# A decoder trunk's block attention: the causal mask added by VectorE, and two query blocks' scores in one stretch

## The chip, the cores and the metric

The kernel runs on one core of a Trainium2 chip. The metric is the device time of one execution in microseconds (us); the median of several executions is compared, and less is better. The core's engines work side by side: TensorE (PE in the profile, its weight loads PEld) multiplies matrices into PSUM; VectorE (DVE) and ScalarE (ACT) do elementwise work and reductions; GpSimd (POOL) and SyncE (SP) mostly issue transfers. Each engine takes its instructions in the order in which the program gives them.

## What is computed

Two layers of a decoder trunk on 512 positions of width 1024. In each, a normalised and modulated input goes through one combined projection; three token mixers follow (pooling, a short convolution, block attention), gated and merged; then an output projection, a second normalisation and a gated feed-forward part. The change is in the block attention: 8 heads of 64, blocks of 256 positions, so a query sees its own block causally, and, if it lies in the second block, the first ("past") block when the routing test admits it:

```python
gate = jnp.einsum('bhqd,bhnd->bhqn', q_i.astype(jnp.float32), kmean)
past = jnp.arange(nb) < blk
gate = jnp.where(past, gate, NEG)
...
s_sel = jnp.where(valid[..., None], s_sel, NEG)
s_own = jnp.where(kpos[None, :] <= qpos[:, None], s_own, NEG)
p = jax.nn.softmax(jnp.concatenate([s_sel, s_own], axis=-1), axis=-1)
```

## The kernel before

TensorE works in a split form: each operand is held as a rounded high part and a low remainder, and `mm3` (L159) issues three matmuls per product. Weights come by DMA as raw tiles (three buffers); ScalarE rounds them to `whi` (L327), VectorE subtracts to get `wlo` (L330), and `next_w` (L351) keeps three or four such pieces ahead of TensorE.

The order of TensorE's work is written out by hand: `matmul` and `transpose` (L150 to L157) keep the program's order. The other engines' instructions are ordered when the program is built, by when their inputs are expected. Side work is woven into the main matmuls by a clock: every 2048 columns of `mm3` are a `tick` (L135), that is four products of 512 columns, twelve main matmuls. At a tick, generators in `fibers` count down and go on, and a queue `bulk` of side tasks gets `bulk_rate` of credit (L906 sets 0.35 for the attention). The tasks there are mostly dots for the modulation (`ada_dot`, L376: a weight row block of 128x1024 times a vector, on VectorE, with one load of 512 KB each).

Attention (`attention`, L661) runs as such a generator beside the gate projections. For each of 4 head pairs it transposes queries and keys (L573) and starts four units, one per 128 queries (`unit`, L580; i is 0 to 3). A unit has three stages:

1. Scores (L584 to L592): a PSUM tile of two banks, one per head (`ps_pair`, two buffers). Two bf16 matmuls of an identity with a mask tile write the mask into the diagonal 128 columns; six matmuls (three split terms, two heads on 64 rows each) add the scores, over 256 columns for units 0 and 1, 384 for unit 2 and 512 for unit 3. Then the softmax on VectorE and ScalarE. For units 0 and 1: maximum (L598), times the scale (L599), two exponentials with sums (L601), reciprocal (L621), scaling of the weights (L623). For units 2 and 3 also the sum over the past block for the routing test (L606 to L608), a maximum over the past (L609) and over the own block (L611), and four exponentials (L616, L618).
2. After `WAIT` ticks (2 for unit 0, else 3): the weights are transposed by TensorE (L632), rounded and split (L634, L635).
3. Two ticks later: the product with the values (L644) and its evacuation (L649 to L654).

The next unit starts `GAP` ticks (2 or 3) after the one before, so two units overlap. With more than 256 keys the third stage's result goes into the unit's own score tile (L641), which is then held until stage 3 has been read.

Of the kernel before, what the change touches and what calls it, by code (L numbers as in the profile page):

```python
# [27 lines left out]
HD = 64  # L28
PAIRS = HEADS // 2
TT = S // P  # L30
# [5 lines left out]
BLOCK = 256  # L36
# [3 lines left out]
NEG = -1e30  # L40
SCALE = 1.0 / math.sqrt(HD)
# [38 lines left out]
def hybrid_trunk(ctx, tc, xT, ws, ada, cols, pool_w, qk_w, crow, pos, con, out):  # L80
    nc = tc.nc
    V, A, T = nc.vector, nc.scalar, nc.tensor

    const = ctx.enter_context(tc.tile_pool(name="const", bufs=1))
# [20 lines left out]

    def ps_pair():
        return psum.tile([P, 2, S], F32, tag="pair", name=nm("pair"), bufs=2)
# [4 lines left out]
    def sm(shape, dt=F32, tag="sm", bufs=8):  # L112
        return small.tile(shape, dt, tag=tag, name=nm(tag), bufs=bufs)
# [8 lines left out]
    bulk_rate, credit = [0.0], [0.0]  # L122
# [27 lines left out]
    def matmul(*a, **k):  # L150
        tc.keep_in_program_order(T.matmul(*a, **k))  # L151
# [44 lines left out]
    ident = const.tile([P, P], F32, name="ident")  # L196
    make_identity(nc, ident)
    ones = const.tile([P, P], F32, name="ones")
    nc.gpsimd.memset(ones, 1.0)
    ident16 = const.tile([P, P], BF16, name="ident16")  # L200
    nc.gpsimd.tensor_copy(ident16, ident)
    mask = const.tile([P, P], BF16, name="mask")
    nc.gpsimd.memset(mask, 0.0)
    nc.gpsimd.affine_select(out=mask, in_=mask, compare_op=ALU.is_ge, fill=NEG,
                            base=0, pattern=[[-1, P]], channel_multiplier=1)
    epst = const.tile([P, 1], F32, name="epst")
    nc.gpsimd.memset(epst, EPS)

    A.activation(csil, csil, AF.Silu)

# [366 lines left out]
    GAP = (2, 3, 3, 3)  # L577
    WAIT = (2, 3, 3, 3)

    def unit(hp, i, q, k, v, y, nrq, prq):  # L580

        w = P * (i + 1)
        wm = max(w, BLOCK)
        s = ps_pair()  # L584

        for a in range(2):
            matmul(s[:, a, i * P:w], ident16, mask, start=True, stop=True)
        for z, (qa, ka) in enumerate(((0, 0), (0, 1), (1, 0))):
            for a in range(2):
                r = slice(a * HD, (a + 1) * HD)  # L590
                matmul(s[:, a, :wm], q[qa][r, i * P:(i + 1) * P], k[ka][r, :wm],
                       start=False, stop=(z == 2), skip_group_check=True)  # L592
        cell = lambda: sm([P, 2], tag="asm", bufs=16)
        nsc, sc = nrq[:, i, 2 * hp:2 * hp + 2], prq[:, i, 2 * hp:2 * hp + 2]
        m, nb, den = cell(), cell(), cell()
        pr = [tmp() for _ in range(2)]
        if w <= BLOCK:
            V.tensor_reduce(m, s[:, :, :w], axis=AX.X, op=ALU.max)  # L598
            V.tensor_mul(nb, m, nsc)  # L599
            for a in range(2):  # L600
                A.activation(pr[a][:, :w], s[:, a, :w], AF.Exp, bias=nb[:, a:a + 1],  # L601
                             scale=sc[:, a:a + 1], accum_out=den[:, a:a + 1])
        else:

            gs, pen, mp, nbp, d2 = cell(), cell(), cell(), cell(), cell()
            V.tensor_reduce(gs, s[:, :, :BLOCK], axis=AX.X, op=ALU.add)  # L606
            V.tensor_mul(gs, gs, sc)
            V.tensor_scalar(pen, gs, NEG * BLOCK * SCALE, NEG, op0=ALU.is_lt, op1=ALU.mult)  # L608
            V.tensor_reduce(mp, s[:, :, :BLOCK], axis=AX.X, op=ALU.max)  # L609
            V.tensor_add(mp, mp, pen)  # L610
            V.tensor_reduce(m, s[:, :, BLOCK:w], axis=AX.X, op=ALU.max)  # L611
            V.tensor_max(m, m, mp)
            V.tensor_mul(nb, m, nsc)
            V.tensor_add(nbp, nb, pen)
            for a in range(2):
                A.activation(pr[a][:, :BLOCK], s[:, a, :BLOCK], AF.Exp, bias=nbp[:, a:a + 1],  # L616
                             scale=sc[:, a:a + 1], accum_out=den[:, a:a + 1])
                A.activation(pr[a][:, BLOCK:w], s[:, a, BLOCK:w], AF.Exp, bias=nb[:, a:a + 1],  # L618
                             scale=sc[:, a:a + 1], accum_out=d2[:, a:a + 1])
            V.tensor_add(den, den, d2)  # L620
        V.reciprocal(den, den)  # L621
# [5 lines left out]
        for aa in ([0, 1],) if i < 2 else ([0], [1]):  # L627
            n = len(aa)
# [17 lines left out]
        c = slice(i * P, (i + 1) * P)  # L646
# [73 lines left out]
    for l in range(L):  # L720
# [7 lines left out]
        for n, (k, lo, hi) in enumerate([(k, 0, S) for k in range(KT)] if l == 0 else HALVES + REST):  # L728
# [17 lines left out]
            w = held[k]  # L746
# [94 lines left out]
        for j in range(2):  # L841
# [8 lines left out]
            z = bigt(F32)  # L850
# [33 lines left out]
        for t in range(TT):  # L884
            for half in range(2):
                src = v_ps[t][:, half * BLOCK:(half + 1) * BLOCK].rearrange("p (n d) -> p n d", d=HD)
                o = v[half][t]
# [15 lines left out]

        if l == 0:
            bulk.extend(ada_tasks(l, (SC2, SH2), True))
        bulk_rate[0] = 0.35  # L906
        ahead_now[0] = 3

        def gate():
# [197 lines left out]
        for part, (along, single, pairs) in enumerate(PARTS):  # L1107
# [18 lines left out]
            for _ in range(single):  # L1126
                wg = next_w()
                g = ps_mm()
                feature_tile(g, wg)
                u = ps_mm()  # L1130
# [135 lines left out]
```

## Time and profile before

| | before |
|---|---|
| median of 3 runs | 1458.94 us (1458.75 to 1459.29) |
| the profiled execution | 1458.56 us, span of its trace 1456.8 us |
| mask matmuls | 64, some 224 ns each from start to end |
| attention stage of layer 0, of layer 1 | from about 134.6 us, from about 851 us |

The profile is one execution. Its span runs from the first to the last instruction of the program; the execution's own time is a little longer. A row of the timeline gives the start in us from the span's start, the length in us, the engine, the source line, the operation, what is written from what, the shape and the number of like instructions that follow each other. TensorE's matmuls are pipelined: a matmul's length is longer than its distance to the next one's start, so costs are read from the distance between starts. All matmuls have one of two lines, L151 (`matmul`) and L157 (`transpose`), so they are told apart by their tiles: `pair<-mask,ident` the mask, `pair<-big,big` on 64 rows the scores, `mm<-ident,tmp` the transposes of weights, `mm<-ident,w` those of queries and keys, `mm<-big,whi` and `mm<-big,wlo` the main matmuls.

### The profile page before, as it was taken

Reading aid. Unit: us, or ns where it says so; the run is one execution under the profiler, and the core shown is the slowest. Engines: PE = TensorE matmul, PEld = TensorE weight load, DVE = VectorE, ACT = ScalarE, POOL = GpSimd, SP = SyncE. Lnnn points to the kernel's source line nnn. Section 1 sums busy time; section 2 is a strip of 40 time slices with the busy share of each in tenths; the row PEclk is TensorE's granted clock in tenths of the full one; section 3 lists DMA queues with packets and bytes.
Section 4 is the critical chain, followed back from the end, with each engine's and each line's share of the span. In section 5 each row is a group of like instructions: output and inputs, shape, how many; then the busy total and the mean of one; then the engine's idle time right before and its main releaser. Section 6 shows DMA issues by size and latency. Waiting matters only on the chain.

```text
span 1456.8 us, 21945 instructions
## 1 busy us (share of the span) xinstructions
PE 1449.7 (100%) x8443; PEld 1267.1 (87%) x8443; DVE 1053.3 (72%) x1855; ACT 665.5 (46%) x1138; POOL 105.9 (7%) x157
## 2 busy tenths in 40 slices
PE   9999999999999999999999999999999999999998
PEld 7888888788989998989988888888889889989997
DVE  7988888748686767677797866776587757657663
ACT  4634555443554452535444355555335525434450
POOL 0000000001100311210000000000010102111200
PEclk9999999999999999999999999999999999999999
DMA  9645334445436666756545422222463436636522
GB/s 352 225 137 173 123 109 137 138 159 142 109 127 211 194 174 203 187 151 199 191 148 177 157 79 73 73 74 101 154 194 88 135 124 164 183 100 190 136 87 84
DMA packets 84409, 217.19 MB, mean 149 GB/s; under 512 B 10832, under 2 KB 23760, under 8 KB 84304
## 3 DMA queue, kind: packets, MB, share of 16 engines
q1 hardware_dynamic: 67456, 177.37, 35.7%
q0 software_dynamic: 16128, 37.76, 11.9%
q8 instruction: 66, 1.08, 0.3%
q10 hardware_dynamic: 720, 0.66, 0.1%
q14 instruction: 39, 0.32, 0.1%
HBM read 213.65 MB, written 2.10 MB: 148 GB/s over the span
## 4 chain that ended last, share of the span: by engine, by line
PE 96%; DMA 2%; DVE 1%; ACT 0%; issue 0%; SPq 0%; POOL 0%
PE mm L151 82%; PE pair L151 13%; PE mm L157 2%; DMA w<-in_ws 1%; DMA w<-in_ada 0%; DMA x<-in_xT 0%; DVE w L376 0%; DVE wlo L330 0%; ACT whi L327 0%; DVE big L504 0%; SPq L190 0%; DVE tmp L497 0%; ACT big L501 0%; DVE w L635 0%; DVE big L702 0%
## 5 line engine op out<-in xcount | busy, mean ns | idle before, releaser
L151 PE MATMUL mm<-big,whi 128*128 128x512 f32 (+1 forms) x4362 | 1079.9, 339 | 0.3 <-DVE w L635 0.2
L151 PEld LDWEIGHTS mm<-big,whi 128*128 128x128 f32 x4362 | 745.3, 190 | 84.8 <-DVE w L635 0.6
L151 PE MATMUL mm<-big,wlo 128*128 128x512 f32 (+1 forms) x2181 | 735.9, 337 | 0.0
L151 PEld LDWEIGHTS mm<-big,wlo 128*128 128x128 f32 x2181 | 413.8, 190 | 44.5
L327 ACT ACTIVATE whi<-raw 128x1024 fp32r<-128x1024 f32 (+2 forms) x240 | 248.8, 1039 | 277.8 <-PE mm L151 193.7
L330 DVE TENSOR_TENSOR wlo<-raw,whi 128x1024 fp32r<-128x1024 f32 (+2 forms) x240 | 283.8, 1192 | 53.7 <-ACT whi L327 53.4
L327 ACT ACTIVATE whi<-w 128x1024 fp32r<-128x1024 f32 x72 | 76.2, 1058 | 149.1 <-PE mm L151 88.7
L958 DVE SCALAR_TENSOR_TENSOR x<-mm,mod,x 128x512 f32<-128x512 f32 (+1 forms) x90 | 61.8, 688 | 79.6 <-PE mm L151 79.5
L256 POOL DMA_DIRECT2D w<-in_ws x72 | 48.2, 678 | 961.7 <-DVE w L376 390.3
L330 DVE TENSOR_TENSOR wlo<-w,whi 128x1024 fp32r<-128x1024 f32 x72 | 86.7, 1220 | 32.0 <-ACT whi L327 31.4
L376 DVE SCALAR_TENSOR_TENSOR w<-w,csil 128x1024 f32<-128x1024 f32 x80 | 95.8, 1219 | 14.0 <-DMA w<-in_ada 13.8
L151 PE MATMUL pair<-whi,big 128*128 128x512 f32 x224 | 76.7, 390 | 0.0
L258 POOL DMA_DIRECT2D w<-in_ws x72 | 64.6, 937 | 152.1 <-DMA w<-in_ws 137.4
L151 PE MATMUL pair<-big,whi 128*128 128x256 f32 (+1 forms) x376 | 74.0, 294 | 0.0
L151 PEld LDWEIGHTS pair<-big,whi 128*128 128x128 f32 x376 | 60.4, 191 | 2.2
L151 PE MATMUL mm<-whi,big 128*128 128x512 f32 x160 | 57.2, 394 | 1.4 <-ACT big L501 1.1
L151 PE MATMUL pair<-big,wlo 128*128 128x256 f32 (+1 forms) x188 | 55.3, 294 | 0.0
L918 DVE SCALAR_TENSOR_TENSOR big<-big,mm 128x512 f32<-128x512 f32 x48 | 32.6, 683 | 26.5 <-PE mm L151 26.1
L151 PEld LDWEIGHTS pair<-whi,big 128*128 128x128 f32 x224 | 42.1, 188 | 8.6
L515 DVE TENSOR_TENSOR big<-tmp,big 128x512 fp32r<-128x512 f32 x48 | 33.1, 691 | 21.7 <-ACT big L514 20.7
L514 ACT ACTIVATE big<-tmp 128x512 fp32r<-128x512 f32 x48 | 29.8, 622 | 35.2 <-DVE tmp L1100 12.8
L151 PE MATMUL pair<-wlo,big 128*128 128x512 f32 x112 | 43.7, 390 | 0.0
(192 smaller groups left out, 1241.1 us busy)
## 6 DMA issues: line engine op xcount, KB each, us to landing
raw<-in_ws SPq DMA_DIRECT2D x146, 512.0 KB, 3.4
w<-in_ada SPq DMA_DIRECT2D x80, 512.0 KB, 4.9
w<-in_ws POOLq DMA_DIRECT2D x144, 256.0 KB, 4.6
raw<-in_ws SPq DMA_DIRECT2D x64, 256.0 KB, 3.9
raw<-in_ws SPq DMA_DIRECT2D x24, 384.0 KB, 3.4
raw<-in_ada SPq DMA_DIRECT2D x16, 512.0 KB, 3.3
raw<-in_ws SPq DMA_DIRECT2D x16, 448.0 KB, 5.5
raw<-in_ws SPq DMA_DIRECT2D x36, 128.0 KB, 2.8
```

The lines of the kernel that those rows point to most:

```text
L151: tc.keep_in_program_order(T.matmul(*a, **k))
L157: tc.keep_in_program_order(T.transpose(*a))
L256: nc.gpsimd.dma_start(dst, self.source(0, 1))
L258: nc.gpsimd.dma_start(dst, self.source(*other), accum_op=ALU.add)
L327: A.activation(hi[:, :n], raw[:, :n], AF.Copy)
L330: ins = V.tensor_sub(lo[:, :n], raw[:, :n], f32(hi)[:, :n])
L376: return V.scalar_tensor_tensor(aw, aw, 1.0, csil, op0=ALU.mult, op1=ALU.mult, accum_out=mod[l][:, part, j:j + 1])
L514: A.activation(hi, src, AF.Copy)
L515: last_split[0] = V.tensor_sub(lo, src, f32(hi))
L918: V.scalar_tensor_tensor(sg, sg, 1.0, branch, op0=ALU.add, op1=ALU.mult)
L958: V.scalar_tensor_tensor(x[k][:, lo:hi], src, mod[l][:, part, k:k + 1], x[k][:, lo:hi], op0=ALU.mult, op1=ALU.add)
```

## The change

The bf16 identity and mask become one f32 mask in SBUF, and a column `fill` with the routing threshold is added. Unit 0 issues the scores of units 0 and 1 in one stretch of twelve matmuls into one pair tile (columns 0 to 255 of each bank for unit 0, 256 to 511 for unit 1), and one VectorE addition puts the mask onto both diagonal blocks. Unit 1 then takes its half of that tile. Units 2 and 3 issue their six score matmuls without the mask; their softmax does the past block's sum, maximum and test first, then adds the mask to the diagonal block, and the own block's exponentials stand ahead of the past's. The bulk rate in the attention goes from 0.35 to 0.27.

```diff
-    ident16 = const.tile([P, P], BF16, name="ident16")
-    nc.gpsimd.tensor_copy(ident16, ident)
-    mask = const.tile([P, P], BF16, name="mask")
+    mask = const.tile([P, P], F32, name="mask")
...
+    fill = const.tile([P, 1], F32, name="fill")
+    nc.gpsimd.memset(fill, NEG * BLOCK * SCALE)
...
-        wm = max(w, BLOCK)
-        s = ps_pair()
-
-        for a in range(2):
-            matmul(s[:, a, i * P:w], ident16, mask, start=True, stop=True)
-        for z, (qa, ka) in enumerate(((0, 0), (0, 1), (1, 0))):
-            for a in range(2):
-                r = slice(a * HD, (a + 1) * HD)
-                matmul(s[:, a, :wm], q[qa][r, i * P:(i + 1) * P], k[ka][r, :wm],
-                       start=False, stop=(z == 2), skip_group_check=True)
+
+        def scores(o, i, n):
+            for z, (qa, ka) in enumerate(((0, 0), (0, 1), (1, 0))):
+                for a in range(2):
+                    r = slice(a * HD, (a + 1) * HD)
+                    matmul(o[:, a], q[qa][r, i * P:(i + 1) * P], k[ka][r, :n], start=(z == 0), stop=(z == 2))
+
+
+        if i == 0:
+            s = first_two[hp] = ps_pair()
+            for u in range(2):
+                scores(s[:, :, u * BLOCK:(u + 1) * BLOCK], u, BLOCK)
+            diag = s.rearrange("p a (g c) -> p a g c", c=P)[:, :, 0:TT:TT - 1]
+            V.tensor_add(diag, diag, mask.unsqueeze(1).unsqueeze(1).to_broadcast([P, 2, 2, P]))
+        elif i == 1:
+            s = first_two.pop(hp)[:, :, BLOCK:]
+        else:
+            s = ps_pair()
+            scores(s[:, :, :w], i, w)
...
-            gs, pen, mp, nbp, d2 = cell(), cell(), cell(), cell(), cell()
-            V.tensor_reduce(gs, s[:, :, :BLOCK], axis=AX.X, op=ALU.add)
-            V.tensor_mul(gs, gs, sc)
-            V.tensor_scalar(pen, gs, NEG * BLOCK * SCALE, NEG, op0=ALU.is_lt, op1=ALU.mult)
-            V.tensor_reduce(mp, s[:, :, :BLOCK], axis=AX.X, op=ALU.max)
-            V.tensor_add(mp, mp, pen)
-            V.tensor_reduce(m, s[:, :, BLOCK:w], axis=AX.X, op=ALU.max)
-            V.tensor_max(m, m, mp)
-            V.tensor_mul(nb, m, nsc)
-            V.tensor_add(nbp, nb, pen)
+            past, own, diag = s[:, :, :BLOCK], s[:, :, BLOCK:w], s[:, :, i * P:w]
+            gs, under, mp, nbp, d2 = cell(), cell(), cell(), cell(), cell()
+            V.tensor_reduce(gs, past, axis=AX.X, op=ALU.add)
+            V.tensor_reduce(mp, past, axis=AX.X, op=ALU.max)
             for a in range(2):
-                A.activation(pr[a][:, :BLOCK], s[:, a, :BLOCK], AF.Exp, bias=nbp[:, a:a + 1],
+                V.scalar_tensor_tensor(under[:, a:a + 1], gs[:, a:a + 1], sc[:, a:a + 1], fill,
+                                       op0=ALU.mult, op1=ALU.is_lt)
+            V.tensor_add(diag, diag, mask.unsqueeze(1).to_broadcast([P, 2, P]))
+            V.scalar_tensor_tensor(mp, under, NEG, mp, op0=ALU.mult, op1=ALU.add)
+            V.tensor_reduce(m, own, axis=AX.X, op=ALU.max)
+            for a in range(2):
+                V.scalar_tensor_tensor(nb[:, a:a + 1], m[:, a:a + 1], mp[:, a:a + 1], nsc[:, a:a + 1],
+                                       op0=ALU.max, op1=ALU.mult)
+            V.scalar_tensor_tensor(nbp, under, NEG, nb, op0=ALU.mult, op1=ALU.add)
+            for a in range(2):
+                A.activation(pr[a][:, BLOCK:w], own[:, a], AF.Exp, bias=nb[:, a:a + 1],
                              scale=sc[:, a:a + 1], accum_out=den[:, a:a + 1])
-                A.activation(pr[a][:, BLOCK:w], s[:, a, BLOCK:w], AF.Exp, bias=nb[:, a:a + 1],
+            for a in range(2):
+                A.activation(pr[a][:, :BLOCK], past[:, a], AF.Exp, bias=nbp[:, a:a + 1],
                              scale=sc[:, a:a + 1], accum_out=d2[:, a:a + 1])
...
-        bulk_rate[0] = 0.35
+        bulk_rate[0] = 0.27
```

More of the change, by code (lines that the diff above doesn't have):

```diff
@@ L578, in hybrid_trunk @@
     WAIT = (2, 3, 3, 3)
+    first_two = {}
     def unit(hp, i, q, k, v, y, nrq, prq):
         w = P * (i + 1)
-        wm = max(w, BLOCK)
-        s = ps_pair()
-        for a in range(2):
-            matmul(s[:, a, i * P:w], ident16, mask, start=True, stop=True)
-        for z, (qa, ka) in enumerate(((0, 0), (0, 1), (1, 0))):
-            for a in range(2):
-                r = slice(a * HD, (a + 1) * HD)
-                matmul(s[:, a, :wm], q[qa][r, i * P:(i + 1) * P], k[ka][r, :wm],
-                       start=False, stop=(z == 2), skip_group_check=True)
+        def scores(o, i, n):
[14 more added lines that the diff above has]
+            scores(s[:, :, :w], i, w)
         cell = lambda: sm([P, 2], tag="asm", bufs=16)
```

## The prediction

> **What bounds the kernel now.** First the profile's page: its span, its busy shares and the chain that ended last; then who TensorE waited for, and the two stretches that hold the attention of the two layers.
>
> ```profile
> span 1456.8 us, 21945 instructions
> PE 1449.7 (100%) x8443; PEld 1267.1 (87%) x8443; DVE 1053.3 (72%) x1855; ACT 665.5 (46%) x1138; POOL 105.9 (7%) x157
> ...
> PE 96%; DMA 2%; DVE 1%; ACT 0%; issue 0%; SPq 0%; POOL 0%
> ...
> PE pair L151 <- POOL ones L199: 1.1, 1, 1.1
> ...
> PE mm L151 <- DVE big L504: 0.2, 1, 0.2
> ...
> 125.00:300.00 175.00, 175.00 (x921) 141.18 (x920) 138.51 (x326) 92.69 (x208) 0.00 (x0) 1.00 0.37 127
> 835.00:1010.00 175.00, 174.80 (x911) 140.62 (x910) 123.31 (x292) 90.51 (x202) 0.00 (x0) 1.00 0.22 78
> ```
>
> The last two rows give, after the stretch and its length, the busy time of PE, PEld, DVE, ACT and POOL, and then the granted clock. TensorE has work in 1449.7 of 1456.8 us, 96% of the chain is TensorE, and the rows of its waits, of which the first and the last of five stand here, run from 1.1 us down to 0.2. In both attentions it never rests. So what leaves TensorE's own sequence leaves the span, as long as nothing that it needs comes late; VectorE has 138.5 of 175 us taken in layer 0 and 123.3 in layer 1, and can take more if it is not in a hurry.
>
> "Busy" is modelled, so I take TensorE's costs from the starts of consecutive matmuls. The rows are start, length, operation, count. One normal step first, then the first head pair's unit 0, unit 1 with unit 0's transposes, and two blocks of transposes that stand alone.
>
> ```profile
> 31.76 2.72 PE mm L151 x12
> ...
> 134.41 0.39 PE L151 MATMUL mm<-big,wlo 128*128 128x512 f32 x1
> 134.64 0.28 PE L151 MATMUL pair<-mask,ident 128*128 128x128 bf16 x2
> 134.85 0.62 PE L151 MATMUL pair<-big,big 64*128 64x256 f32 x6
> 135.40 0.74 PE L151 MATMUL mm<-big,whi 128*128 128x512 f32 x2
> 135.98 0.40 PE L151 MATMUL mm<-big,wlo 128*128 128x512 f32 x1
> ...
> 140.79 0.39 PE L151 MATMUL mm<-big,wlo 128*128 128x512 f32 x1
> ...
> 141.78 0.44 PE L157 MATMUL mm<-ident,tmp 128*128 128x128 f32 x2
> 141.98 0.71 PE L151 MATMUL mm<-big,whi 128*128 128x512 f32 x2
> 142.52 0.39 PE L151 MATMUL mm<-big,wlo 128*128 128x512 f32 x1
> ...
> 160.87 0.96 PE L151 MATMUL pair<-big,big 64*128 64x512 f32 x6
> 161.76 0.87 PE L157 MATMUL mm<-ident,tmp 128*128 128x128 f32 x6
> ...
> 164.98 0.39 PE L151 MATMUL mm<-big,wlo 128*128 128x512 f32 x1
> 165.21 0.60 PE L157 MATMUL mm<-ident,w 128*128 128x128 f32 x4
> 165.57 0.70 PE L151 MATMUL mm<-big,whi 128*128 128x512 f32 x2
> 166.10 0.39 PE L151 MATMUL mm<-big,wlo 128*128 128x512 f32 x1
> ...
> 172.29 1.03 PE L157 MATMUL mm<-ident,tmp 128*128 128x128 f32 x8
> 173.08 0.71 PE L151 MATMUL mm<-big,whi 128*128 128x512 f32 x2
> ```
>
> A main matmul takes 2.72/12 = 0.227 us. An interruption costs what lies between its neighbours beyond one step, and what the next two main matmuls take beyond 0.45:
> - unit 0 (mask and 6 score matmuls): 135.40-134.41-0.23 = 0.76, and 0.58-0.45 = 0.13; together 0.89.
> - unit 1 with unit 0's 2 transposes: 141.98-140.79-0.23 = 0.96, and 0.09; 1.05.
> - the two mask matmuls: 134.85-134.64 = 0.21.
> - six more score matmuls of 256 columns: the six at 512 take 161.76-160.87 = 0.89, those at 256 take 0.55; 256 more columns in each cost 0.34 (the two heads' row halves run side by side, so this is three streams, 0.113 each).
> - transposes alone: four cost 165.57-164.98-0.23 = 0.36 and 0.08 after them, 0.44; eight take 173.08-172.29 = 0.79 ahead of that tail (from a main matmul to the first transpose is a normal step, 164.98 to 165.21). So 0.11 each, and two cost 0.44-0.22 = 0.22.
>
> **The change, part by part.**
>
> (1) The mask leaves TensorE: 32 units lose two matmuls, 0.21 us each. Not all of it need be gained, as three rows of the timeline show, in which single matmuls are cut out of the groups above:
>
> ```profile
> 134.71 0.22 PE L151 MATMUL pair<-mask,ident 128*128 128x128 bf16 x1
> 134.85 0.38 PE L151 MATMUL pair<-big,big 64*128 64x256 f32 x2
> ...
> 135.19 0.28 PE L151 MATMUL pair<-big,big 64*128 64x256 f32 x2
> ```
>
> From the second mask matmul to the first scores are 0.14 to 0.15 us, where one mask matmul follows the other after 0.07: some 0.09 passes with nothing streaming. From the last scores to the next main matmul (135.40) are 0.21, against a stream of 0.11: again 0.09 to 0.10. From a main matmul to the mask are 0.23, a normal step: nothing is lost. The lost 0.09 comes where the array goes from 128 rows to 64 or back, not where the type changes. After the change a main matmul (128 rows) is followed by scores (64 rows), a pairing that the trace doesn't have. Its cost beyond a normal step lies between 0 (a stream of 0.227 us cannot be cut short) and, if the scores need all that the mask now takes, 0.21; I take the 0.09 of the two nearest rows. The gain is then 0.21-0.09 = 0.12 per unit, 0.21 at one end and 0 at the other. The Trainium skill, TensorEngine Tiling (Array Packing), section Tiling Modes, says that changing the tiling mode drains TensorE; by that rule the mask bears a cost now that the scores will bear afterwards, the trace agrees with its 0.09 us at both changes of rows, and the sum below would be 6.8 us; without the rule, 9.0.
>
> (2) Unit 1's scores move into unit 0's stretch. Before, units 0 and 1 with unit 0's transposes cost 0.89+1.05 = 1.94 us per head pair. After: one stretch of 0.89-0.21+0.09+0.34 = 1.11 and two transposes alone, 0.22: 1.33. That is 0.61 less (0.70 without the 0.09), masks included, for 8 head pairs: 4.9 us (5.6). Units 2 and 3 gain by (1) alone: 16 times 0.12 = 1.9 us (16 times 0.21 = 3.4). TensorE's sequence is **6.8 us** shorter (9.0; and if the scores took all 0.21, 8 times 1.94-(0.89+0.34+0.22) = 3.9).
>
> (3) VectorE takes the mask, and here a wait can arise: the transposes of a unit's weights wait for L623, and TensorE runs in order, so whatever stands behind them waits too. The nearest rows for the new additions are VectorE's additions out of PSUM; below them, unit 0's chain with its exponentials on ScalarE, and the tightest chain, of a unit 3.
>
> ```profile
> 143.08 0.41 DVE L635 TENSOR_TENSOR w<-mm,w 128x256 fp32r<-128x256 f32 x1
> 153.56 0.68 DVE L635 TENSOR_TENSOR w<-mm,w 128x512 fp32r<-128x512 f32 x1
> ...
> 135.71 1.22 DVE L376 SCALAR_TENSOR_TENSOR raw<-raw,csil 128x1024 f32<-128x1024 f32 x1
> 136.86 0.42 DVE L598 TENSOR_REDUCE asm<-pair 128x2 f32<-128x256 f32 x1
> 137.31 0.16 DVE L599 TENSOR_TENSOR asm<-asm,nrq 128x2 f32<-128x2 f32 x1
> ...
> 137.60 0.45 ACT L601 ACTIVATE tmp<-pair,asm,nrq 128x128 f32<-128x128 f32 x1
> 138.38 0.21 ACT L601 ACTIVATION_READ_ACCUMULATOR tmp<-pair,asm,nrq 128x1 f32 x1
> ...
> 139.22 0.48 DVE L623 TENSOR_SCALAR tmp<-tmp,asm 128x128 f32<-128x128 f32 x2
> ...
> 256.14 0.88 DVE L623 TENSOR_SCALAR tmp<-tmp,asm 128x512 f32<-128x512 f32 x2
> 256.79 1.04 PE L157 MATMUL mm<-ident,tmp 128*128 128x128 f32 x8
> ```
>
> Units 0 and 1: one addition over 512 elements, 0.68 us. Units 2 and 3: one over 256, 0.41 us. The rest of the softmax keeps its two or three reductions; small operations of 0.15 to 0.17 are exchanged for about as many (multiply, test, add, maximum, multiply, add: 6; now 2 tests, 2 combined updates, 2 combined maxima: 6). VectorE gains 4(0.68+2 times 0.41) = 6 us per layer, 138.5 to some 145 of 170. That hides as long as each chain meets its deadline.
>
> Unit 0's deadline comes closer from two sides. Its chain grows by 0.68, and, in the order in which the changed program's instructions stand on VectorE, unit 1's maximum (512 elements, as many as the addition, so 0.6 to 0.7) comes ahead of unit 0's L623; and unit 1's scores no longer stand ahead of unit 0's transposes on TensorE (0.76, as 134.64 to 135.40 for unit 0's; 0.34 of it is now spent in the stretch before). For the first head pair, whose L623 ends at 139.70 against transposes at 141.78, a margin of 2.1 us: in the new order a dot (L376, 135.71 to 136.86, 1.15) also stands between its maximum and L599. Addition 136.86 to 137.56, maximum to 138.0, dot to 139.2, L599 to 139.4, the exponentials, as now about 1.0 from the first's start to the second's sum (137.60 to 138.59), to 140.45, reciprocal 140.6, unit 1's maximum 141.2, L623's first half 141.5. TensorE arrives at about 141.78-0.61 = 141.2. That is a stall of 0.3 to 0.5 us. The three other pairs of layer 0 have no such dot at that place, and I expect none there.
>
> Units 2 and 3 have three ticks of main matmuls (3 times 2.72 us) for their chain. The tightest of the 32 blocks of transposes is in the third pair: the first half of L623 ends at about 256.14+0.44 = 256.6, the transposes start at 256.79: 0.2 us to spare. Their chain grows by 0.41, but the lower rate (part 5) takes one dot of 1.15 out of just this stretch in the new order. For it and the next tightest I allow 0.2 us in all. Stalls: **0.6 us**. The bounds: 0, as now; and 3.8, if all eight units 2 and 3 of layer 0 paid their whole growth (3.3) on top of unit 0's 0.5.
>
> (4) The own block's exponentials ahead of the past's: the same four instructions, ScalarE (92.7 of 175 us) has room; the first starts when nb is there, one operation of 0.16 earlier. Costed at nothing; without that room it is 0.16 in 16 units, 2.6 us, and only where a unit has no margin.
>
> (5) The bulk rate: 16 dots stand in layer 0's attention now. At 0.27 for 0.35 all 16 still come before the flush behind the gates in the new order, the last three some 25 to 30 us later than now, in stretches with no unit. They and their loads are the same in number, and no transfer is added; SyncE's queue is only passed in another order. Nothing.
>
> ```profile
> L376 DVE SCALAR_TENSOR_TENSOR raw<-raw,csil x16: 1211/1216/1226, 133.4 to 276.8; 128x1024 f32<-128x1024 f32 x16
> ```
>
> (6) Pair tiles: three instead of four are taken per head pair from two buffers. The next pair's first scores need unit 2's tile, as they do now, and unit 3's the one of units 0 and 1, read long before. Nothing. POOL builds one constant less a copy, at the start: nothing.
>
> Sum: -6.8+0.6 = -6.2 us on the profiled execution's 1458.56 (its span 1456.8 and 1.8 around it): 1452.4. The median, 1458.94, lies 0.4 above that execution, so I put the median at **1452.6**. About 0.2% (2.9 us) is what a measurement of this kernel can tell from no change.
>
> **Rivals.**
> - *No drain without the mask* (chance 0.22): a main matmul passes into scores as it now passes into the mask, in one step. For it: 134.41 to 134.64 is a normal step. Against it: both changes of rows in the trace lose 0.09. Then -9.0+0.6: 1450.5 (1449.9 without stalls).
> - *The chain eats a part* (0.17): VectorE's order puts a weight split or a dot of 1.2 us into one chain after the other, in layer 0 above all. For it: the margin of 0.2 us and unit 0 above. Against it: layer 1 has no dots there. With 2 to 4 us of stalls 1454.1 to 1456.1.
> - *Slower* (0.06): TensorE waits at the transposes of almost every unit of layer 0, as every wait of VectorE for an exponential also holds up the weight splits queued behind it, and these the next unit. For it: VectorE's queue is in order. To lose 6.8 and 2.9 more, growth has to exceed the margin by 9.7/16 = 0.6 us in each of the 16 units; the first pair's unit 0, with its 2.1, would have to grow by 2.7, against 1.3 and a dot worked out. It decides where VectorE's queue is full (layer 0); then 1462 or more.
> - *The mask's time gives nothing* (0.05): the scores' weights are loaded in the 0.21 us that the mask takes and would need them anyway. For it: the load of a score's weights begins only there. Only the joined stretches are gained, 3.9-0.6: 1455.6; and with the chain eating as above 1457 to 1459.
>
> **How the numbers follow.** Forecast 0.50 (1451.5 to 1453.5), no drain 0.22, partly eaten 0.17, mask's time not gained 0.05, slower 0.06. The range goes from the gain without drain and stalls (1458.9-9.0 = 1449.9, and 0.4 for the spread of the runs, 1449.5) to the bound of 3.8 us of stalls, 1455.9; no more than the last two cases and a little lies outside. Faster by over 0.2% (under 1456.0): 0.50+0.22 and 0.15 of the third, 0.87; within 0.2% 0.07; slower by over 0.2% 0.06.
>
> **What would show it.** No row of mask and ident on TensorE; from a main matmul to the first scores 0.32 us between starts (forecast) or 0.23 (no drain); the stretch of 12 scores costing 1.1 us and two transposes alone 0.22; TensorE's waits with a row for VectorE's L623 of about 0.6 us in layer 0. A sum of those waits of 3 us and more, or idle TensorE in layer 1's attention, would make it wrong.

## The result, and the profile after

The changed kernel takes **1453.05 us** (median of 6 runs, 1452.58 to 1454.23), the kernel before 1458.74 us (6 runs, 1458.61 to 1459.29): a ratio of 0.9961, 95% interval 0.9948 to 0.9974. The forecast was 1452.6, the range 1449.5 to 1455.9. The profiled execution took 1453.40 us.

The profile's page of the changed kernel: span, busy shares, and the chain that ended last by engine.

```profile
span 1451.6 us, 21853 instructions
...
PE 1443.5 (99%) x8379; PEld 1263.2 (87%) x8379; DVE 1062.9 (73%) x1879; ACT 664.0 (46%) x1138; POOL 105.5 (7%) x157
...
PE 95%; DVE 2%; DMA 1%; ACT 1%; issue 0%; SPq 0%; ACTq 0%
```

PE has 8379 matmuls where it had 8443, the 64 of the mask less, and is still the bound. VectorE's part of the chain went from 1% to 2%. Whom TensorE waited for (us in all, times, longest):

```profile
...
PE mm L157 <- DVE w L651: 0.8, 1, 0.8
...
```

This row is new: a transpose (L157) waited 0.8 us for L651, which is the split of transposed weights (L635 before). There is none for L639, the scaling of the weights (L623 before), the place where I had looked for the stalls. The same two stretches as before, busy time of PE, PEld, DVE, ACT, POOL:

```profile
125.00:300.00 175.00, 174.20 (x898) 141.07 (x897) 142.21 (x333) 92.04 (x209) 0.00 (x0) 1.00 0.36 121
835.00:1010.00 175.00, 174.91 (x896) 141.53 (x895) 128.72 (x310) 91.81 (x211) 0.00 (x0) 1.00 0.24 82
```

In layer 0 TensorE now rests for 0.8 of 175 us. VectorE took up 5.4 us in layer 1 (123.3 to 128.7) and 3.7 in layer 0; 6 were forecast. In layer 0 the lower rate moved two dots, 2.5 us, to behind the end of this stretch (the last dot starts at 313.4 for 276.8), so 6.2 came there too. Now the timeline of TensorE and VectorE: the joined stretch, the addition of the mask, the first pair's unit 0, and the place of the new wait.

```profile
134.79 0.39 PE L151 MATMUL mm<-big,wlo 128*128 128x512 f32 x1
135.11 0.97 PE L151 MATMUL pair<-big,big 64*128 64x256 f32 x12
136.01 0.74 PE L151 MATMUL mm<-big,whi 128*128 128x512 f32 x2
136.59 0.40 PE L151 MATMUL mm<-big,wlo 128*128 128x512 f32 x1
137.20 0.70 DVE L598 TENSOR_TENSOR pair<-pair,mask 128x512 f32<-128x512 f32 x1
...
141.29 0.47 DVE L639 TENSOR_SCALAR tmp<-tmp,asm 128x128 f32<-128x128 f32 x2
141.40 0.39 PE L151 MATMUL mm<-big,wlo 128*128 128x512 f32 x1
141.62 0.52 PE L157 MATMUL mm<-ident,tmp 128*128 128x128 f32 x2
141.91 0.71 PE L151 MATMUL mm<-big,whi 128*128 128x512 f32 x2
...
162.24 1.22 DVE L376 SCALAR_TENSOR_TENSOR raw<-raw,csil 128x1024 f32<-128x1024 f32 x1
163.38 0.69 DVE L618 TENSOR_REDUCE asm<-pair 128x2 f32<-128x512 f32 x1
163.99 0.68 DVE L619 TENSOR_REDUCE asm<-pair 128x2 f32<-128x512 f32 x1
164.58 0.34 DVE L621 SCALAR_TENSOR_TENSOR asm<-asm,nrq,fill 128x1 f32<-128x1 f32 x2
164.66 0.39 PE L151 MATMUL mm<-big,wlo 128*128 128x512 f32 x1
164.84 0.42 DVE L623 TENSOR_TENSOR pair<-pair,mask 128x256 f32<-128x256 f32 x1
165.24 0.55 DVE L651 TENSOR_TENSOR w<-mm,w 128x384 fp32r<-128x384 f32 x1
165.84 0.66 PE L157 MATMUL mm<-ident,w 128*128 128x128 f32 x4 [0.80 <-DVE w L651]
```

From the main matmul to the first scores are 135.11-134.79 = 0.32 us, the forecast's number. The stretch of twelve costs 136.01-134.79-0.23 = 0.99, and 0.58-0.45 = 0.13 after it: 1.12, forecast 1.11. Unit 0's transposes cost 141.91-141.40-0.23 = 0.28 ahead of their tail, against 0.14 to 0.15 where they don't wait: 0.14 us of stall. The query transposes of the next pair start 165.84-164.66 = 1.18 us behind their main matmul, where a normal step is 0.23: **0.95 us** lost.

To compare whole blocks, I count from the start of the main matmul ahead of an interruption to the start of the eighth behind it and take eight normal steps of 0.2267 us off. Medians over the 8 head pairs of both layers, in us:

| block | before | after |
|---|---|---|
| scores of unit 0 | 0.919 | 1.145 (units 0 and 1) |
| scores of unit 1 with unit 0's two transposes | 1.080 | 0.253 (transposes alone) |
| scores of unit 2 with four transposes | 1.461 | 1.334 |
| scores of unit 3 with six transposes | 1.839 | 1.713 |
| sum per pair | 5.299 | 4.445 |

The difference is 0.854 us per pair, 6.8 us for eight: the forecast's sum. The blocks of one kind in the table differ by at most 0.01 us, except where one waits. What waits, beyond its kind's median: the query transposes 1.0 (0.95 by the single rows above) and, at 839.9, 0.26; the block with the key transposes at 965.4 0.10; unit 0's 0.14; the eight transposes at 927.5 0.28, whose block lost 0.47 before. Net of that 0.47 the new waits come to 1.3 us. 6.8-1.3 = 5.5 lies between the difference of the spans, 5.2, and that of the medians, 5.7. The rest lies ahead of both attentions: TensorE is already 0.24 us later in the changed kernel's trace at 117.6. Nor is the 0.26 at 839.9 a price of the mask: it stands ahead of layer 1's first unit, and the same place loses 0.29 in the trace of experiment 7 below, which leaves the mask on TensorE.

### The profile page after: what moved, and what is told of

It is laid out like the page before. It is cut to its first block, busy times and chain, and to the rows that moved or that the text cites. A ratio compares the mean times of both kernels' runs of the same rounds, so it can differ in the third digit from the quotient of the medians.

```text
span 1451.6 us, 21853 instructions
## 1 busy us (share of the span) xinstructions
PE 1443.5 (99%) x8379; PEld 1263.2 (87%) x8379; DVE 1062.9 (73%) x1879; ACT 664.0 (46%) x1138; POOL 105.5 (7%) x157
## 4 chain that ended last, share of the span: by engine, by line
PE 95%; DVE 2%; DMA 1%; ACT 1%; issue 0%; SPq 0%; ACTq 0%
PE mm L151 81%; PE pair L151 13%; PE mm L157 2%; DVE raw L376 0%; DMA w<-in_ada 0%; DMA x<-in_xT 0%; DVE wlo L330 0%; DMA raw<-in_ws 0%; DVE w L376 0%; DVE big L504 0%; ACT whi L327 0%; DVE big L934 0%; DVE big L518 0%; DVE tmp L639 0%; DVE asm L618 0%
## 5 line engine op out<-in xcount | busy, mean ns | idle before, releaser
L330 DVE TENSOR_TENSOR wlo<-raw,whi 128x1024 fp32r<-128x1024 f32 (+2 forms) x240 | 283.7, 1192 | 50.0 <-ACT whi L327 49.6
L330 DVE TENSOR_TENSOR wlo<-w,whi 128x1024 fp32r<-128x1024 f32 x72 | 86.7, 1220 | 31.8 <-ACT whi L327 31.1
L376 DVE SCALAR_TENSOR_TENSOR w<-w,csil 128x1024 f32<-128x1024 f32 x80 | 95.9, 1219 | 14.0 <-DMA w<-in_ada 14.0
## 6 DMA issues: line engine op xcount, KB each, us to landing
w<-in_ws POOLq DMA_DIRECT2D x144, 256.0 KB, 4.6
raw<-in_ws SPq DMA_DIRECT2D x64, 256.0 KB, 3.8
```

The source lines that it names most:

```text
L330: ins = V.tensor_sub(lo[:, :n], raw[:, :n], f32(hi)[:, :n])
L376: return V.scalar_tensor_tensor(aw, aw, 1.0, csil, op0=ALU.mult, op1=ALU.mult, accum_out=mod[l][:, part, j:j + 1])
```

## The experiments

Each was timed in five rounds beside the kernel before, which had medians of 1458.75 to 1459.05 us. They were timed in four sets (1 to 4, 5 to 8, 9 and 10, 11 and 12), so a difference of 0.3 us between experiments of two sets says nothing.

| experiment | median (range), us | ratio to before, 95% |
|---|---|---|
| 1 changed, bulk rate 0.35 | 1451.84 (1451.55 to 1452.09) | 0.9950 (0.9938 to 0.9962) |
| 2 before, no mask | 1454.99 (1454.61 to 1455.42) | 0.9972 (0.9961 to 0.9982) |
| 3 before, scores joined | 1455.82 (1455.54 to 1456.74) | 0.9979 (0.9970 to 0.9988) |
| 4 before, mask on VectorE | 1459.01 (1458.26 to 1459.31) | 0.9999 (0.9990 to 1.0007) |
| 5 changed at 0.35, units apart | 1454.93 (1454.63 to 1455.76) | 0.9973 (0.9962 to 0.9983) |
| 6 changed at 0.35, old softmax | 1457.55 (1456.34 to 1458.45) | 0.9989 (0.9980 to 0.9997) |
| 7 before, new softmax | 1459.13 (1458.81 to 1459.50) | 1.0001 (0.9992 to 1.0010) |
| 8 changed at 0.35, past's exponentials first | 1453.45 (1453.16 to 1453.86) | 0.9962 (0.9950 to 0.9975) |
| 9 changed at 0.35, mask added first | 1453.29 (1452.85 to 1455.06) | 0.9964 (0.9950 to 0.9978) |
| 10 changed at 0.35, old small steps | 1455.03 (1454.15 to 1456.33) | 0.9975 (0.9965 to 0.9985) |
| 11 changed, bulk rate 0.20 | 1452.28 (1452.17 to 1453.44) | 0.9958 (0.9944 to 0.9971) |
| 12 changed, bulk rate 0.45 | 1455.81 (1454.78 to 1457.06) | 0.9979 (0.9970 to 0.9988) |

My theory behind the first four: TensorE's sequence gives all that was counted, with the drain at the change of rows, and the waits come from the order of work on VectorE. The rivals are those of the prediction: no drain, or the mask's time gives nothing.

### What leaves TensorE: experiments 2 and 3

Experiment 2, on the kernel before (its output lacks the causal mask):

```diff
-        for a in range(2):
-            matmul(s[:, a, i * P:w], ident16, mask, start=True, stop=True)
...
-                       start=False, stop=(z == 2), skip_group_check=True)
+                       start=(z == 0), stop=(z == 2))
```

> The kernel before without the 64 mask matmuls and with no mask anywhere: the causal mask is left out of the computation, and each score group starts with its first matmul. VectorE and ScalarE have what they had. Theory (the change of rows loses 0.09 us, and the scores bear it once the mask is gone): 32 units times 0.125 = 4.0 us less, 1454.7; from the last main matmul to the first scores 0.32 us. Rival (no drain at a main matmul followed by scores): 32 times 0.215 = 6.9 us less, 1451.9, and 0.23 us. Second rival (the scores' weight loads hide under the mask): 1458.7.

1459.05-1454.99 = 4.06 us for 32 units: 0.127 each. The theory of a loss at the change of rows holds, both rivals fall. TensorE's timeline without the mask shows where the other 0.08 us of the mask's 0.21 stay:

```profile
134.49 0.39 PE L151 MATMUL mm<-big,wlo 128*128 128x512 f32 x1
134.81 0.62 PE L151 MATMUL pair<-big,big 64*128 64x256 f32 x6
```

0.32 us again instead of 0.23: the change from 128 to 64 rows now happens between the main matmul and the scores. What TensorE does in these 0.09 us no row shows; "drain" is a name for them here. The rule of the Trainium skill that I had weighed (TensorEngine Tiling (Array Packing), section Tiling Modes: a change of tiling mode drains TensorE) agrees with these rows.

Experiment 3 joins the two stretches and leaves the mask on TensorE and the softmax as it was:

```diff
+        if i == 0:
+            s = first_two[hp] = ps_pair()
+            stretch(s, (0, 1), BLOCK)
+        elif i == 1:
+            s = first_two.pop(hp)[:, :, BLOCK:]
```

> The kernel before with units 0 and 1 in one stretch and nothing else: four mask matmuls, then the twelve score matmuls, in one pair tile; softmax, mask on TensorE and rate as before. Theory (one entry and one exit of 64 rows fewer per head pair): per head pair 0.89+0.13+0.34 = 1.36 us and two transposes alone 0.25, against 1.94 to 2.00: 0.36 to 0.39 less, 2.9 to 3.1 us for eight, 1455.7 if unit 0's transposes don't wait; they now come 0.8 us sooner, with 2.1 us to spare at the first pair. Rival (the columns streamed are what counts, and these are the same): 1458.7.

3.2 us, a little over the 2.9 to 3.1 expected. In the blocks of its trace units 0 and 1 take 1.379+0.261 = 1.64 us per pair for 0.919+1.080 = 2.00 before, 0.36 less, 2.9 for eight. 4.06+3.23 = 7.3, and experiment 1 gains 1459.05-1451.84 = 7.2: the two parts add up. The blocks give 6.8 for the same; the medians of the kernel before, 1458.74 with the result and 1459.05 here, differ by nearly as much.

### The bulk rate: experiments 1, 11 and 12

```diff
-        bulk_rate[0] = 0.27
+        bulk_rate[0] = 0.35
```

> The changed kernel with the bulk rate back at 0.35. In the changed kernel TensorE waits 0.8 us at 165.8 us for a split of transposed weights on VectorE (L651), and a dot (L376, 1.15 us) stands in VectorE's queue ahead of that split. Theory: the dot, placed there by the rate 0.27, is the cause; without it the split ends at about 164.6 us, ahead of TensorE, the row of the wait goes, and the median falls by about 0.9 us, to 1452.1. Rival: the longer softmax chain itself makes the split late; then the wait stays at 0.8 us and the median at 1453.

1451.84: the rest of the change is worth 1.2 us more without the new rate. The slowest execution here is faster than the fastest at 0.27 (1452.09 against 1452.58), though the two intervals of the ratios overlap. The same place in the kernel before, then TensorE and VectorE in experiment 1:

```profile
162.87 0.56 DVE L635 TENSOR_TENSOR w<-mm,w 128x384 fp32r<-128x384 f32 x1
```

```profile
164.42 0.55 DVE L651 TENSOR_TENSOR w<-mm,w 128x384 fp32r<-128x384 f32 x1
164.60 0.39 PE L151 MATMUL mm<-big,wlo 128*128 128x512 f32 x1
165.02 0.66 PE L157 MATMUL mm<-ident,w 128*128 128x128 f32 x4
```

The query transposes need a PSUM tile that this split still reads. Before, it started at 162.87, 2.3 us ahead of them. In the new order it stands behind two reductions, two tests and the mask addition, and starts at 164.42: 0.19 us are lost (165.02-164.60-0.23). At 0.27 a dot (162.24 above) stands ahead of all these, the split starts at 165.24, and 0.95 are lost. Is it the rate, or where one dot falls? In the order of VectorE's instructions a dot stands ahead of this first reduction at 0.27 and at 0.45, but at neither 0.20 nor 0.35. So I ran 0.20 and 0.45 (the diff is the same line):

> The changed kernel with bulk rate 0.20 (0.27 measured 1453.05 us, 0.35 measured 1451.84). Theory A, only the place of single dots counts: at 0.27 a dot of 1.2 us stands on VectorE ahead of the first head pair's unit 3, so that the split of unit 2's transposed weights comes late and holds the PSUM tile that the next pair's query transposes need (0.96 us). At 0.20 no dot stands ahead of any unit 3's first reduction: 1451.6 to 1452.4. Rival B, the lower rate as such costs (dots are pushed behind the attention and meet other work there): 0.20 is slower than 0.27, 1453.5 to 1455.

> The changed kernel with bulk rate 0.45. Theory A, the place counts: as at 0.27 a dot stands on VectorE ahead of the first pair's unit 3 (and another one inside the last pair's unit 3 ahead of its splits), so the query transposes near 165 us wait for the split again, about 1 us: 1452.7 to 1454. Rival B, a higher rate is better because dots are out of the way sooner: 1451 to 1451.9, and no wait at the query transposes.

0.20 gives 1452.28 and no such wait, 0.45 gives 1455.81 and it is back. The place decides; the rate only moves dots. The traces bear this out by layer. From the first scores to the last transposes, layer 0's attention takes 161.09, 162.01, 161.29 and 165.11 us at 0.20, 0.27, 0.35 and 0.45; layer 1's, in which no dot stands, takes 161.25 to 161.27 at all four. So 0.7 of the 1.3 us between the spans at 0.27 and 0.35 belong to layer 0's attention; 0.26 are the wait at 839.9, 0.25 lie behind both attentions, and nothing here ties these two to the rate. In timeline and waits of experiment 12:

```profile
162.29 1.22 DVE L376 SCALAR_TENSOR_TENSOR raw<-raw,csil 128x1024 f32<-128x1024 f32 x1
...
165.90 0.66 PE L157 MATMUL mm<-ident,w 128*128 128x128 f32 x4 [0.95 <-DVE w L651]
```

```profile
PE mm L157 <- DVE tmp L639: 1.5, 2, 1.3
...
```

0.45 was slower than either theory had it: TensorE waits at more places, above all 1.3 us at the six transposes of the third pair (L639). Which dot causes each of these waits was not followed up.

### What pays for the mask: experiments 4 to 7

Experiment 4 only moves the mask: the kernel before, apart as it was, with the old softmax behind one addition per unit.

```diff
-        for a in range(2):
-            matmul(s[:, a, i * P:w], ident16, mask, start=True, stop=True)
...
+        diag = s[:, :, i * P:w]
+        V.tensor_add(diag, diag, mask.unsqueeze(1).to_broadcast([P, 2, P]))
```

> The kernel before with the mask added by VectorE ahead of each unit's softmax and nothing else: 32 additions of 256 elements, units apart, order of the softmax and rate as before. Theory: TensorE's sequence is 4.0 us shorter as without any mask, and the 0.41 us per unit mostly fits into the margins: 1454.7 to 1455.5, with waits of TensorE of under 1 us in all. Rival (the chain through VectorE sets the end): each of the 32 units pays 0.41 less its margin; at no margin that is 13 us, 1467; if only layer 0 pays, about 1458.

A miss: 1459.01, no gain at all. TensorE's sequence is as short as in experiment 2, and all 4 us come back as waits: 1.78 and 1.77 at the eight transposes of the third pair's unit 3 in both layers (256.0 and 972.5), 0.5 at 213.7, 0.1 at 960.9 (the 0.47 that the kernel before lost in layer 1's second pair shrinks by 0.2). Waits, then VectorE, ScalarE and TensorE in the third pair of layer 0:

```profile
PE mm L157 <- DVE tmp L623: 3.2, 2, 1.6
```

```profile
249.24 0.68 DVE L611 TENSOR_REDUCE asm<-pair 128x2 f32<-128x512 f32 x1
249.84 0.15 DVE L610 TENSOR_TENSOR asm<-asm,asm 128x2 f32<-128x2 f32 x1
249.91 1.22 DVE L330 TENSOR_TENSOR wlo<-raw,whi 128x1024 fp32r<-128x1024 f32 x1
251.04 0.15 DVE L612 TENSOR_TENSOR asm<-asm,asm 128x2 f32<-128x2 f32 x1
251.12 0.74 DVE L518 SCALAR_TENSOR_TENSOR big<-mm,colt,big 128x512 fp32r<-128x512 f32 x1
251.78 0.15 DVE L613 TENSOR_TENSOR asm<-asm,nrq 128x2 f32<-128x2 f32 x1
251.84 1.22 DVE L376 SCALAR_TENSOR_TENSOR raw<-raw,csil 128x1024 f32<-128x1024 f32 x1
...
252.99 0.15 DVE L614 TENSOR_TENSOR asm<-asm,asm 128x2 f32<-128x2 f32 x1
...
253.57 0.56 ACT L616 ACTIVATE tmp<-pair,asm,nrq 128x256 f32<-128x256 f32 x1
...
```

The small steps between the own maximum (L611) and the exponentials take 0.15 us each, but foreign work stands between them: a weight split of 1.22 (L330), a split of queries or keys of 0.74 (L518), a dot of 1.22 (L376). From the maximum's end (249.84) to the first exponential (253.57) pass 3.7 us, and the scaling of the weights starts at 257.37. So each dependent step costs what is queued ahead of it, not what it takes itself. Dots are not needed for this: layer 1 has none, and loses as much. There the same four steps stood close together in the kernel before:

```profile
967.05 0.15 DVE L610 TENSOR_TENSOR asm<-asm,asm 128x2 f32<-128x2 f32 x1
967.24 0.16 DVE L612 TENSOR_TENSOR asm<-asm,asm 128x2 f32<-128x2 f32 x1
967.44 0.16 DVE L613 TENSOR_TENSOR asm<-asm,nrq 128x2 f32<-128x2 f32 x1
967.63 0.16 DVE L614 TENSOR_TENSOR asm<-asm,asm 128x2 f32<-128x2 f32 x1
```

In experiment 4 the first of them comes at 967.50, 0.45 later, but the last at 970.10, 2.5 later: a split of queries or keys (L518, 0.74), a weight split (L330, 1.22) and a gate's product (L918, 0.68) now stand between them. The new theory: the mask pays only with a softmax that has fewer such steps. Experiment 5 is experiment 4 with the new softmax (that is, the changed kernel at 0.35 with units 0 and 1 apart, each with its own addition), experiment 6 the changed kernel at 0.35 with the old one behind the addition:

```diff
-        if i == 0:
-            s = first_two[hp] = ps_pair()
...
+        s = ps_pair()
```

> The mask added by VectorE, units apart, rate 0.35, and the changed kernel's softmax (past block's work ahead of the mask, combined updates, own block's exponentials first). With the old softmax the same kernel took 1459.0 us, as the 4.0 us that TensorE saved came back as waits of 3.2 us and more at the transposes of two units 3, whose first exponential stood behind four small steps of VectorE with foreign work of 0.7 to 1.2 us queued between them. Theory (the new softmax has two steps between the own block's maximum and the first exponential, so less foreign work gets between, and the waits go): 1455.0, with waits at those transposes of under 0.3 us. Rival (it was the joined stretch that kept the changed kernel from these waits): 1459.0 again.

```diff
+            diag = s[:, :, i * P:w]
+            V.tensor_add(diag, diag, mask.unsqueeze(1).to_broadcast([P, 2, P]))
+            gs, pen, mp, nbp, d2 = cell(), cell(), cell(), cell(), cell()
+            V.tensor_reduce(gs, s[:, :, :BLOCK], axis=AX.X, op=ALU.add)
+            V.tensor_mul(gs, gs, sc)
```

> The changed kernel (joined stretch, mask on VectorE) at rate 0.35, with the old softmax for units 2 and 3, the mask added ahead of it. Theory (the old softmax makes the first exponential late): two transposes of units 3 wait again, some 3.5 to 4.2 us in all, 1455.3 to 1456. Rival (the joined stretch is what helps): 1451.8, as with the new softmax.

5 came as expected, 1454.93: 4.1 us less than 4, as much as the mask is worth on TensorE. 6 went the expected way and further: 1457.55, 5.7 us above experiment 1, beyond the 1455.3 to 1456 of the theory; the waits are again at the scaling (L636 there: three, 3.4 us in all, the longest 1.6).

Experiment 7, the kernel before with nothing but the new softmax:

```diff
+            V.scalar_tensor_tensor(nbp, under, NEG, nb, op0=ALU.mult, op1=ALU.add)
...
-                A.activation(pr[a][:, BLOCK:w], s[:, a, BLOCK:w], AF.Exp, bias=nb[:, a:a + 1],
+            for a in range(2):
+                A.activation(pr[a][:, :BLOCK], past[:, a], AF.Exp, bias=nbp[:, a:a + 1],
```

> The kernel before with the new softmax for units 2 and 3 alone; mask on TensorE, units apart, rate 0.35. Theory: TensorE's sequence is unchanged and had next to no waits at the transposes, so there is nothing to gain: 1459.0, within 0.5 us. Rival (a shorter chain is worth time in itself): 1457 or less.

1459.13: by itself it gains nothing, since in the kernel before TensorE has no wait for the scaling of the weights (L623) that it could shorten.

### Which part of the softmax: experiments 8, 9 and 10

8 puts the past's exponentials first again, 9 adds the mask ahead of the past's reductions, 10 keeps the order and takes the old small steps:

```diff
-                A.activation(pr[a][:, BLOCK:w], own[:, a], AF.Exp, bias=nb[:, a:a + 1],
+                A.activation(pr[a][:, :BLOCK], past[:, a], AF.Exp, bias=nbp[:, a:a + 1],
```

> The changed kernel at rate 0.35 with the past block's exponentials ahead of the own block's again; all else as in the changed kernel. The first exponential then waits for one more small step, which stands behind a weight split of 1.2 us on VectorE. Theory (it is the number of dependent steps ahead of the first exponential that counts, and one more costs a split of 1.2 us in a chain that has 0.9 us to spare): the tightest unit 3 waits 0 to 0.4 us, 1451.8 to 1452.3. Rival (the exponentials' order is what saves the chain): the waits of 3 to 4 us are back, 1455 to 1456.

```diff
+            V.tensor_add(diag, diag, mask.unsqueeze(1).to_broadcast([P, 2, P]))
             V.tensor_reduce(gs, past, axis=AX.X, op=ALU.add)
```

> The changed kernel at bulk rate 0.35 (1451.84 us), with the mask of units 2 and 3 added ahead of the past block's sum and maximum instead of behind the test. Theory A, the dependent steps decide and not where the one 0.42 us addition stands: 1451.5 to 1452.5. Rival B, the addition's place is what keeps the chains on time (the past's maximum and test in front of it): the 0.42 us are then in front of the whole chain of units 2 and 3, and with the third pairs' blocks of eight transposes 0.2 us from their limit I expect waits of TensorE for the scaled weights and 1453 to 1455.

```diff
-                V.scalar_tensor_tensor(nb[:, a:a + 1], m[:, a:a + 1], mp[:, a:a + 1], nsc[:, a:a + 1],
-                                       op0=ALU.max, op1=ALU.mult)
+            V.tensor_max(m, m, mp)
+            V.tensor_mul(nb, m, nsc)
```

> The changed kernel at bulk rate 0.35 (1451.84 us), same order (past's sum and maximum, test, mask, own maximum, own exponentials first), but with the old kernel's small steps: product and test, addition, maximum, product, addition, each over both heads, in place of the combined steps. Between the two kernels that differ in the whole softmax lie 5.7 us, of which the exponentials' order alone gave 1.6. Theory A, each dependent small step is queued behind foreign work of 0.7 to 1.2 us, and the old form has one more of them between the own maximum and the first exponential: most of the other 4.1 comes back as waits for the scaled weights at the third pairs' eight transposes, 1454 to 1456. Rival B, the order alone decides: 1451.5 to 1452.5.

8: 1453.45, between the two theories and in neither's range, 1.6 us above experiment 1. It loses 0.9 at the first pair's block of unit 3's scores and unit 2's six transposes (160.2), which I hadn't named, and nothing at the third pair's unit 3. VectorE and ScalarE at unit 2 in experiment 8, then ScalarE's first exponential there in experiment 1:

```profile
157.18 0.35 DVE L627 SCALAR_TENSOR_TENSOR asm<-asm,asm,nrq 128x1 f32<-128x1 f32 x2
157.44 1.22 DVE L330 TENSOR_TENSOR wlo<-raw,whi 128x1024 fp32r<-128x1024 f32 x1
158.58 0.16 DVE L629 SCALAR_TENSOR_TENSOR asm<-asm,asm 128x2 f32<-128x2 f32 x1
158.77 0.56 ACT L631 ACTIVATE tmp<-pair,asm,nrq 128x256 f32<-128x256 f32 x1 [3.70 <-DVE asm L629]
```

```profile
157.18 0.46 ACT L631 ACTIVATE tmp<-pair,asm,nrq 128x128 f32<-128x128 f32 x1 [2.37 <-DVE asm L627]
```

The past's exponentials need L629, the own ones only L627, and between the two stands a split: own first means 1.3 us earlier here, not 0.16 (158.77 against 157.18, less 0.25 by which L627 itself stands later in experiment 8).

9: 1453.29, in the interval of the rival (1453 to 1455), so the addition's place is worth about 1.4 us; but not where the rival put it. No eight transposes wait; four blocks of query transposes lose 0.25 us each (206.4, 248.1, 878.6, 920.3). There the own maximum (L625) comes ahead of the first split (L651), which then holds the PSUM tile, as at 164.66 above.

10: 1455.03, in theory A's interval: 3.2 us above experiment 1 with the order unchanged. The eight transposes wait again, 1.2 us at 255.1, 0.6 at 213.1 and 0.6 at 928.3 (0.29 there in experiment 1). VectorE and ScalarE in the third pair, experiment 10, then the two rows of experiment 1 that answer to them:

```profile
247.96 0.68 DVE L624 TENSOR_REDUCE asm<-pair 128x2 f32<-128x512 f32 x1
248.56 1.21 DVE L330 TENSOR_TENSOR wlo<-raw,whi 128x1024 fp32r<-128x1024 f32 x1
249.69 0.15 DVE L625 TENSOR_TENSOR asm<-asm,asm 128x2 f32<-128x2 f32 x1
249.76 0.74 DVE L518 SCALAR_TENSOR_TENSOR big<-mm,colt,big 128x512 fp32r<-128x512 f32 x1
250.42 0.15 DVE L626 TENSOR_TENSOR asm<-asm,nrq 128x2 f32<-128x2 f32 x1
250.60 0.57 ACT L629 ACTIVATE tmp<-pair,asm,nrq 128x256 f32<-128x256 f32 x1 [1.05 <-DVE asm L626]
```

```profile
247.33 0.68 DVE L625 TENSOR_REDUCE asm<-pair 128x2 f32<-128x512 f32 x1
...
249.17 0.56 ACT L631 ACTIVATE tmp<-pair,asm,nrq 128x256 f32<-128x256 f32 x1
```

Maximum and scaling as two steps let a weight split (L330) and a split of queries or keys (L518) in: 2.6 us from the maximum's start to the first exponential instead of 1.8. The three parts alone give 1.6, 1.4 and 3.2 us, 6.2 in all against the 5.7 of the whole softmax. They cost at different places, so the sum is a comparison of sizes and not an account.

## Why the prediction was right, and where it was not

- **(1) and (2), TensorE's sequence: right, in sum and in mechanism.** 6.8 us forecast, 6.8 measured. The loss at the change of rows stays (0.32 us to the first scores); without it the mask would have given 0.21 per unit, experiment 2 gives 0.127. By part it holds too: 0.60 us per pair for units 0 and 1 (0.61 forecast) and 0.13 each for units 2 and 3 (0.12).
- **(3) The additions on VectorE: right in size** (0.70 and 0.42 for 0.68 and 0.41), **wrong as to what waits.** 0.6 us of stalls were forecast at L623, now L639: 0.3 to 0.5 at the first pair's unit 0 and 0.2 at the third pair's unit 3. Measured: 0.14 at the first, none at the second, and 1.3 more than before in all, most of it elsewhere. That the forecast still came within 0.5 us of the median is in part luck: its 0.6 stood for waits that hardly came, in place of waits that it had not named. "In both attentions it never rests" had passed over a sign. Among the rows of waits of the kernel before is one more:

```profile
PE mm L151 <- DVE w L635: 0.2, 1, 0.2
```

It is a main matmul in layer 1's attention (933.83) that waits for the split of transposed weights. So before the change this split already held up TensorE once, and it is the instruction that the query transposes wait for now.
- **(5) "The bulk rate: nothing" is the step that was wrong.** It asked whether a dot comes late for the end of the attention, not what each dot now stands in front of. One stands ahead of unit 3's reductions, and so of the split whose PSUM tile the next query transposes need: 0.95 us there (0.19 with the old rate), and 1.2 us between the medians of experiment 1 and the changed kernel, of which the traces put 0.7 into layer 0's attention.
- **(4) "Costed at nothing" held as a term, but for the wrong reason, so by luck.** The order and the combined steps are no trifle of 0.16 us: without the new softmax the change keeps 1.4 of its 7.2 us (experiment 6). Counted against the old softmax they gain nothing (experiment 7) because TensorE did not wait for that scaling then. For units 2 and 3 I had taken the growth of a chain as the sum of its own operations (0.41), and in this queue it grows by what gets in between.
- **(6) The pair tiles: right.** In all 24 stretches of scores the first one starts 0.32 to 0.33 us behind its main matmul, so none waited for a tile.
- **The chances.** "The chain eats a part" happened in small, 1.3 us rather than 2 to 4. That it could have eaten everything is shown by experiment 4; its mechanism is the one I had put down as the slower rival, splits and dots queued around the chain, and it decided in a few tight places rather than in sixteen units. "Layer 1 has no dots there", put down against it, was no protection: experiment 4 loses 1.78 us in layer 0 and 1.77 in layer 1.

Experiment 1 is the fastest version here: the change with the old bulk rate, 1451.84 us. What stays open: whether the last small waits (0.1 to 0.3 us each) could be avoided by placing single instructions by hand wasn't tried.

## What to carry to other kernels

Take the bound engine's sequence from the distances between starts and the sum can come out to a tenth of a microsecond, but only as long as every deadline of the other engines holds; so list, for each instruction that the change moves, which buffer it frees and who takes that buffer next. On an engine shared with long side work, a chain's length is its number of dependent steps times what may be queued between them (here 0.7 to 1.2 us), so merge steps before adding one. A knob that only shifts side work in time is no free edit: look at what each shifted piece lands in front of.

## What the runs showed of the hardware

- Going from matmuls of 128 rows to some of 64 costs 0.08 to 0.09 us at both places where it was put: 0.32 us instead of 0.23 from a main matmul to the first scores, with and without the mask addition (changed kernel and experiment 2), and 0.15 instead of 0.07 from the second mask matmul to them (kernel before). On the way back the last scores take 0.20 us to the next main matmul instead of 0.11, in all three.
- A block of TensorE work that doesn't wait costs the same to 0.01 us in all eight head pairs of the two layers (the kinds in the table), so waits of 0.1 us can be read off one trace.
- A wait can be longer than the row that names it: the query transposes stand 0.95 us late, and the profile puts 0.80 of that down to L651.
